# Retention's heads and memory attention's queries and keys turned by transposing DMAs in place of TensorE, and the first key group rotated earlier

## The chip, the cores and the metric

The kernel runs on one core of one Trainium2 chip. A core has TensorE (PE in the profile: matrix products; PEld are its weight loads), VectorE (DVE), ScalarE (ACT), GpSimd (POOL) and SyncE (SP), which here only issues DMAs; 16 DMA engines move data between the device's memory (DRAM) and the on-chip memory (SBUF). Products land in a small accumulator memory (PSUM). The metric is the device time of one execution in microseconds (us); lower is better.

## The reference, cut to what matters

One decoder layer on 256 tokens of width 2048 in float32. The parts that the change touches are the retention mixer's heads on their way into a projection, and the queries and keys of the attention over 256 memory tokens:

```python
hn = rmsnorm(h, norm_mix_w)
q, k, v, g_ret, xr, yr, g_a, g_b = jnp.split(hn @ w_in, offsets, axis=-1)
q = rotary(q, positions); k = rotary(k, positions) * RET_QK_DIM ** -0.5      # 8 heads of 128
ret = head_groupnorm(chunkwise_retention(q, k, v), ret_gn_w).reshape(b, s, D_RET_V)
ret_out = jax.nn.silu(g_ret) * ret                                            # 8 heads of 256
rnn_out = jax.nn.gelu(yr) * rg_lru(causal_dwconv(xr, ...), ...)
merged = sigmoid(g_a) * (ret_out @ w_proj_ret) + sigmoid(g_b) * (rnn_out @ w_proj_rnn)
h = h + merged @ w_mix_out
# attention over the memory, 4 heads of 512
q = rmsnorm(h, norm_xa_w) @ xa_w_q;  k = mem_n @ xa_w_k;  v = mem_n @ xa_w_v
p = softmax(q k^T * 512 ** -0.5);    h = h + (p v) @ xa_w_o
hn = rmsnorm(h, norm_ffn_w); h = h + (silu(gate) * val) @ ffn_w_down          # a causal conv before the gate
out = rmsnorm(h, final_norm_w)
```

## The kernel before, in words

**Precision.** Each float32 operand is split in two parts, hi (a cast) and lo (the remainder, operand minus hi), and a product is hi*hi + hi*lo + lo*hi. ScalarE makes hi of each piece of weights (L285), VectorE makes lo (L286). `split_pair` (L543) does the same for activations, two blocks of 128 features at a time.

**Weights.** All weights come from DRAM as one stream of 1 MB pieces, `in_wall`, in the order of a plan. `prefetch` issues the load of a piece on SP (L264) into one of six raw buffers, and the splits into one of three hi and three lo buffers; it stays two units (`AHEAD`) ahead of the products. In a projection with two blocks of 512 columns (`pair_products`), some products are saved by adding pieces of weights and of activations first: a second piece is added to a raw buffer by a DMA on GpSimd (L266) or by VectorE, and the products read sums of activations (`ss`, made by `sums`). Such a pair has eleven units, seven short ones (q1 to q7, 12 matmuls) and four long ones (p0 to p3, 24 matmuls). Other projections go by four long units.

**Order.** The program is written once in straight order. `later(n, fn)` puts a piece of side work n+1 units later; after each unit those that are due are written out. A scheduler then places instructions on each engine; every engine, and SP's queue, works in order, so one that waits holds what stands behind it.

**Rows and columns.** A projection with `pair_out` gives rows (tokens on partitions), and an operand of the next product must have features on partitions. `transposed` (L523) turns 128x128 blocks on TensorE with an identity matrix (`cid`), four at a time into a PSUM tile `sm` (L529). It is used for:

- retention's heads: `finish_head` (L747) turns a normalised head `rc` (256 tokens x 256), scales it by the group norm's weights into `hd` (L752), and stores it to DRAM; `ret`, a list of the class `Kept`, loads each pair of blocks again (`kt`, L739) while the gates of the merge are computed, splits it, and for the first four also makes the sums that the pair projection needs;
- the queries: `keep` (L1118) turns `o`, copies it to `qc` (L1121), and stores it to DRAM (`qs`, also `Kept`), to be loaded as `kt` before the softmax;
- the keys: `turn_key` (L1135) turns `o` and splits straight out of PSUM (L547, L548 with `sm` as the input), and asks for the softmax two units after the second half;
- the merged rows (`sig` and `o` of the gates) and the residual rows (`nat`), which stay.

**Group 0 of retention.** Queries and keys of four heads are computed with features on partitions, joined (`q`, L540), and rotated by position on VectorE (`rotated`, L715 to L721, then `split_pair`). For group 0, keys: the sums of x (`sum_x`) are put into the four units of the value projection that follows, then comes that projection, and the rotation is written after it, before the values are split (`split_rows`, L562 and L563). The score products (`scores`, L517, `sm<-s,s`) read the rotated keys.

Of the kernel before, what the change touches and what calls it, by code (L numbers as in the profile page):

```python
# [9 lines left out]
F32 = mybir.dt.float32  # L10
F32R = mybir.dt.float32r
I32 = mybir.dt.int32
AF = mybir.ActivationFunctionType
ALU = mybir.AluOpType
AX = mybir.AxisListType

P = 128
D = 2048
S = 256
# [134 lines left out]
def hybrid_layer(  # L154
# [37 lines left out]
    def tmp(s="t"):  # L192
        return tp.tile([P, 2, S], F32, tag="tmp", name=nm(s))
# [109 lines left out]
    def later(n, fn):  # L303

        pending.append((step[0] + n + 1, fn))
# [217 lines left out]
    def transposed(rows):  # L523

        for k in range(0, rows.shape[2], 2 * P):
            t = small()
            for j in range(2):
                for tt in range(2):
                    pe.transpose(  # L529
                        t[:, j, tt * P : (tt + 1) * P], rows[:, tt, k + j * P : k + (j + 1) * P], ident  # L530
                    )
            yield t
# [175 lines left out]
    def rotated(qs_):  # L708

        o = []  # L710
        cb = cos[:, None, :].to_broadcast([P, 2, S])
        for pr in range(2):
            q = qs_[pr]
            ta, tb = tmp("ta"), tmp("tb")
            dve.tensor_tensor(out=ta, in0=q, in1=cb, op=ALU.mult)  # L715
            for lo_, hi_ in ((0, 64), (64, 128)):
                dve.tensor_tensor(  # L717
                    out=tb[lo_:hi_], in0=q[64 - lo_ : 128 - lo_],
                    in1=sin[64 - lo_ : 128 - lo_, None, :].to_broadcast([64, 2, S]), op=ALU.mult,
                )  # L720
            dve.tensor_add(ta, ta, tb)  # L721
            o.append(split_pair(ta))
        return o

    class Kept(list):
# [4 lines left out]
        def store(self, t):  # L730

            sp.dma_start(out=self.rows[self.stored], in_=t)
            self.stored += 1
# [8 lines left out]
                    self.sums.append(sums(t, self.scale))  # L742
            return list.__getitem__(self, i)

    ret = Kept("ret")

    def finish_head(g, hh, raw):  # L747
        for t in transposed(raw):
            c = tmp("hd")
            for j in range(2):  # L750
                i = g * 8 + hh * 2 + j
                act.activation(c[:, j, :], t[:, j, :], AF.Identity, scale=half_gn[:, i : i + 1])  # L752
            ret.store(c)

    def retain(g, qr, kr, vs, dec, gates):

# [73 lines left out]
    for g in range(2):  # L830
        dec = big([P, 4, S], s="dec")
        vs, turned = [], []
        for b, o in enumerate((O_Q, O_K)):
            a = qjoin if g == b == 0 else [joined(t, "q") for t in gemm_t("w_in", 0, xs, NT, o + g * BW)]
            if b == 0:
                sp.dma_start(
                    out=dec,
                    in_=consts[:, C_DEC + g * 4 * S : C_DEC + (g + 1) * 4 * S].rearrange("p (h s) -> p h s", s=S),
                )
            if g > 0:  # L840
                turned.append(rotated(a))
# [271 lines left out]
        done[0] += 1  # L1113
        act.copy(pT, t)

    qs = Kept("qs", None, False)

    def keep(o, pr, kept):  # L1118
        for t in transposed(o[:, :, pr * S : (pr + 1) * S]):
            c = tmp("qc")  # L1120
            act.copy(c, t)  # L1121
            kept.store(c)
# [12 lines left out]
    def turn_key(b, o, pr, ks):  # L1135
        for t in transposed(o[:, :, pr * S : (pr + 1) * S]):
            ks.append(split_pair(t))
        if pr == 1:
            later(1, lambda: softmax([qs[2 * b], qs[2 * b + 1]], ks))

    for b in (0, 2):
        for i in range(KC):
            later(4 + 2 * i, lambda i=i: qs[2 * b + i])
        for i, o in enumerate(pair_out("xa_w_k", ms, ms.sums, b * BW, rsms[0])):
            ks = []
            for pr in range(2):
                later(1 + 3 * i + pr, lambda b=b + i, o=o, pr=pr, ks=ks: turn_key(b, o, pr, ks))
    osp, osp_sums = [], []

    def attend(b, v):  # L1150
# [194 lines left out]
```

## Time and profile before

| | |
|---|---|
| median of 3 runs | 2006.2 us (2006.16 to 2008.58) |
| the profiled execution's own time | 2005.55 us |
| its span in the profile | 2003.8 us |
| granted TensorE clock | 0.999 |
| moved by DMA | 443.57 MB, 221 GB/s over the span |

In a group's row stand the line, engine, operation, output<-input by the program's names, partitions x elements, the count, then busy us and the mean ns of one, then the engine's idle time before them and what ended it. In a timeline's row stand the start, the busy time, the engine, the line and, in brackets, the idle time before it and what ended that. Matmuls overlap: one of 512 columns lasts about 0.39 us and the next starts 0.23 us after it began. A DMA row has its size and the median time from issue to landing. A stretch's row has its length, then the busy us (and count) of PE, PEld, DVE, ACT and POOL, the clock, the mean busy share of the DMA engines, and GB/s.

### The profile page before, as it was taken

Reading aid. Unit: us, or ns where it says so; the run is one execution under the profiler, and the core shown is the slowest. Engines: PE = TensorE matmul, PEld = TensorE weight load, DVE = VectorE, ACT = ScalarE, POOL = GpSimd, SP = SyncE. Lnnn points to the kernel's source line nnn. Section 1 sums busy time; section 2 is a strip of 40 time slices with the busy share of each in tenths; the row PEclk is TensorE's granted clock in tenths of the full one; section 3 lists DMA queues with packets and bytes.
Section 4 is the critical chain, followed back from the end, with each engine's and each line's share of the span. In section 5 each row is a group of like instructions: output and inputs, shape, how many; then the busy total and the mean of one; then the engine's idle time right before and its main releaser. Section 6 shows DMA issues by size and latency. Waiting matters only on the chain.

```text
span 2003.8 us, 24972 instructions
## 1 busy us (share of the span) xinstructions
PE 1988.4 (99%) x10072; PEld 1692.9 (84%) x10072; DVE 1583.4 (79%) x1588; ACT 1157.9 (58%) x1167; POOL 47.0 (2%) x52
## 2 busy tenths in 40 slices
PE   9999999999999999999999999999999999999998
PEld 8878888888888888888888888888888888888887
DVE  6798797789985876778888768777797787886775
ACT  6565656767665554566666656555554554544552
POOL 0001000000000000000000000000000000000000
PEclk9999999999999999999999999999999999999999
DMA  9764675555887675777886748754678555684561
GB/s 370 259 214 135 235 257 179 210 190 157 266 261 261 210 252 183 248 257 234 267 259 206 258 126 231 264 198 174 207 233 275 196 192 216 204 290 178 204 237 64
DMA packets 79460, 443.57 MB, mean 221 GB/s; under 512 B 8688, under 2 KB 13424, under 8 KB 31600
## 3 DMA queue, kind: packets, MB, share of 16 engines
q1 hardware_dynamic: 72064, 397.39, 53.9%
q0 software_dynamic: 5760, 41.95, 11.2%
q10 hardware_dynamic: 1520, 2.63, 0.4%
q8 instruction: 79, 1.29, 0.3%
q14 instruction: 37, 0.30, 0.0%
HBM read 425.16 MB, written 16.78 MB: 221 GB/s over the span
## 4 chain that ended last, share of the span: by engine, by line
PE 91%; DVE 3%; issue 2%; DMA 2%; ACT 1%; POOLq 0%; SPq 0%; ACTq 0%; POOL 0%; DVEq 0%
PE acc L350 38%; PE acc L361 16%; PE acc L368 16%; PE acc L362 16%; DMA raw<-in_wall 2%; PE sm L517 2%; DVE lo L286 1%; PE sm L529 1%; PE acc L517 1%; ACT hi L285 1%; PE sm L894 1%; DVE raw L293 0%; DVE tb L717 0%; DVE ta L721 0%; DVE fv L1192 0%
## 5 line engine op out<-in xcount | busy, mean ns | idle before, releaser
L286 DVE TENSOR_TENSOR lo<-raw,hi 128x2048 fp32r<-128x2048 f32 (+1 forms) x420 | 951.0, 2267 | 295.0 <-ACT hi L285 288.1
L285 ACT CAST hi<-raw 128x2048 fp32r<-128x2048 f32 (+1 forms) x418 | 793.2, 1902 | 615.5 <-PE acc L362 274.2
L361 PE MATMUL acc<-hi,s 128*128 128x512 f32 x1336 | 522.6, 391 | 2.0 <-DVE v L563 1.6
L362 PE MATMUL acc<-hi,s 128*128 128x512 f32 x1336 | 520.7, 390 | 0.4 <-DVE s L551 0.4
L350 PE MATMUL acc<-s,hi 128*128 128x512 f32 x2176 | 519.3, 392 | 1.1 <-DVE hi L283 1.1
L350 PEld LDWEIGHTS acc<-s,hi 128*128 128x128 f32 x2176 | 402.7, 189 | 80.9 <-issue 1.4
L368 PE MATMUL acc<-lo,s 128*128 128x512 f32 x1336 | 340.0, 392 | 0.0
L361 PEld LDWEIGHTS acc<-hi,s 128*128 128x128 f32 x1336 | 250.9, 188 | 54.6 <-DVE v L563 2.0
L368 PEld LDWEIGHTS acc<-lo,s 128*128 128x128 f32 x1336 | 250.1, 188 | 53.3
L362 PEld LDWEIGHTS acc<-hi,s 128*128 128x128 f32 x1336 | 250.9, 188 | 52.2 <-DVE s L551 1.1
L350 PEld LDWEIGHTS acc<-s,lo 128*128 128x128 f32 x2176 | 277.7, 192 | 8.8 <-DVE lo L286 0.4
L350 PE MATMUL acc<-s,lo 128*128 128x256 f32 x2176 | 282.9, 284 | 0.0
L361 PE MATMUL acc<-hi,ss 128*128 128x512 f32 x320 | 126.4, 395 | 1.8 <-ACT o L453 1.5
L362 PE MATMUL acc<-hi,ss 128*128 128x512 f32 x320 | 124.8, 390 | 0.0
L368 PE MATMUL acc<-lo,ss 128*128 128x512 f32 x320 | 86.0, 390 | 0.0
L539 ACT COPY c<-acc 128x512 f32<-128x512 f32 x68 | 39.4, 581 | 70.3 <-PE acc L350 69.9
L361 PEld LDWEIGHTS acc<-hi,ss 128*128 128x128 f32 x320 | 60.1, 188 | 16.0 <-ACT o L453 2.0
L266 POOL DMA_DIRECT2D raw<-in_wall x40 | 35.2, 879 | 1570.3 <-DVE lo L286 999.0
L368 PEld LDWEIGHTS acc<-lo,ss 128*128 128x128 f32 x320 | 60.0, 188 | 12.7
L362 PEld LDWEIGHTS acc<-hi,ss 128*128 128x128 f32 x320 | 60.1, 188 | 12.1
L426 DVE TENSOR_TENSOR nat<-nat,acc 128x512 f32<-128x512 f32 (+1 forms) x49 | 43.9, 908 | 5.1 <-PE acc L368 5.1
L291 DVE TENSOR_TENSOR raw<-raw,raw 128x2048 f32<-128x2048 f32 x20 | 45.8, 2288 | 0.4
(233 smaller groups left out, 1241.8 us busy)
## 6 DMA issues: line engine op xcount, KB each, us to landing
raw<-in_wall SPq DMA_DIRECT2D x333, 1024.0 KB, 4.9
raw<-in_wall POOLq DMA_DIRECT2D x40, 1024.0 KB, 7.9
fkept<-nat SPq DMA_DIRECT2D x12, 512.0 KB, 7.5
nat<-fkept SPq DMA_DIRECT2D x12, 512.0 KB, 5.8
xt<-in_x_t SPq DMA_DIRECT2D x11, 256.0 KB, 6.5
raw<-in_wall SPq DMA_DIRECT2D x5, 512.0 KB, 7.9
nat<-in_x ACTq DMA_DIRECT2D x4, 512.0 KB, 10.0
ret<-hd SPq DMA_DIRECT2D x8, 256.0 KB, 4.1
```

The costliest lines, as they stand in the source:

```text
L266: pool.dma_start(out=raw, in_=src, accum_op=ALU.add)
L285: act.copy(hi[:, a:b], raw[:, a:b])
L286: dve.tensor_tensor(out=lo[:, a:b], in0=raw[:, a:b], in1=hi[:, a:b].bitcast(F32), op=ALU.subtract)
L291: dve.tensor_tensor(out=to, in0=to, in1=by, op=ALU.add)
L350: pe.matmul(a, part, sx, start=k == 0 and t == 0, stop=k == nk - 1 and t == 0, skip_group_check=True)
L361: pe.matmul(o, h, hi, start=start and kk == 0, stop=False, skip_group_check=True)
L362: pe.matmul(o, l, hi, start=False, stop=False, skip_group_check=True)
L368: pe.matmul(o, h, lo, start=False, stop=stop and kk == KC - 1, skip_group_check=True)
L426: dve.tensor_tensor(out=o, in0=o, in1=i, op=op)
L517: pe.matmul(o, a, b, start=start and i == 0, stop=stop and i == 2, skip_group_check=True)
L529: pe.transpose(t[:, j, tt * P : (tt + 1) * P], rows[:, tt, k + j * P : k + (j + 1) * P], ident)
L539: act.copy(c, a[:, :, S:BW])
```

## The change

A float32 word is treated as two 16-bit halves. `planes` writes rows as two planes of halves, upper and lower, by two ScalarE copies of 16-bit values with a stride of two; a transposing DMA (`dma_start_transpose`, issued on SP) turns 128-column blocks of 16-bit values; `join_planes` puts the halves of two blocks together again with two ScalarE copies.

- Heads and queries: a new class `KeptRows` stores the planes of 512 columns (512 KB) to DRAM, and its first use of an even index loads and turns 512 KB at once into a tile `d`; two joins make two pairs of blocks. For the heads, the scaling by the group norm's weights moves behind the join (on ScalarE, in place).
- Keys: the planes are turned within the SBUF, in two transposing DMAs of 128 tokens each; the two joins come three and four units after the planes, the softmax five.
- Group 0: `rotated` for the keys is written before the sums of x and the value projection.

```diff
+    def words(t):
+        return t.bitcast(U16).rearrange("p t (w two) -> p t w two", two=2)
+    def planes(t, rows, cs=slice(0, BW)):
+        for i in range(2):
+            act.copy(t[:, :, i, cs], words(rows)[:, :, :, 1 - i])
+    def join_planes(d, pr):
+        t = tmp("jp")
+        for i in range(2):
+            act.copy(words(t)[:, :, :, 1 - i], d[:, i, 2 * pr : 2 * pr + 2, :])
+        return t
+    class KeptRows(list):
...
+        def store(self, b, t):
+            sp.dma_start(
+                out=self.rows[b].rearrange("(t p) c -> p t c", p=P), in_=t.rearrange("p t a w -> p t (a w)")
+            )
+        def __getitem__(self, i):
+            while len(self) <= i:
+                k = len(self)
+                if k % 2 == 0:
+                    self.turned = big([P, 2, KC, S], U16, s="d")
+                    sp.dma_start_transpose(
+                        out=self.turned.rearrange("p a c s -> p (a c) s"), in_=self.rows[k // 2]
+                    )
+                t = join_planes(self.turned, k % 2)
+                if self.wcol is not None:
+                    for j in range(2):
+                        act.activation(t[:, j, :], t[:, j, :], AF.Identity, scale=self.wcol(2 * k + j))
+                self.append(split_pair(t))
+                if self.wcol is not None and len(self) <= KC:
+                    self.sums.append(sums(t))
...
     def finish_head(g, hh, raw):
-        for t in transposed(raw):
-            c = tmp("hd")
-            for j in range(2):
-                i = g * 8 + hh * 2 + j
-                act.activation(c[:, j, :], t[:, j, :], AF.Identity, scale=half_gn[:, i : i + 1])
-            ret.store(c)
+        if hh % 2 == 0:
+            head_rows[0] = big([P, 2, 2, BW], U16, s="hr")
+        planes(head_rows[0], raw, slice((hh % 2) * DV, (hh % 2 + 1) * DV))
+        if hh % 2 == 1:
+            ret.store(2 * g + hh // 2, head_rows[0])
...
                 if b == 1:
+                    turned.append(rotated(a))
                     for i in range(KC):
                         later(i, lambda i=i: sum_x(i))
                 v = gemm_n("w_in", 0, xs, NT, O_V + b * BW)
-                turned.append(rotated(a))
+                if b == 0:
+                    turned.append(rotated(a))
                 vs.append(split_rows(v, rs0))
...
-            for pr in range(2):
-                later(1 + 2 * i + pr, lambda o=o, pr=pr: keep(o, pr, qs))
+            later(1 + 2 * i, lambda b=b + i, o=o: qs.store(b, row_planes(o)))
...
-    def turn_key(b, o, pr, ks):
-        for t in transposed(o[:, :, pr * S : (pr + 1) * S]):
-            ks.append(split_pair(t))
-        if pr == 1:
-            later(1, lambda: softmax([qs[2 * b], qs[2 * b + 1]], ks))
+    def turn_key(b, o):
+        rows = row_planes(o)
+        d = big([P, 2, KC, S], U16, s="d")
+        for tt in range(2):
+            sp.dma_start_transpose(
+                out=d.rearrange("p a c s -> p (a c) s")[:, :, tt * P : (tt + 1) * P],
+                in_=rows[:, tt].rearrange("p a w -> p (a w)"),
+            )
+        ks = []
+        for pr in range(2):
+            later(2 + pr, lambda pr=pr: ks.append(split_pair(join_planes(d, pr))))
+        later(4, lambda: softmax([qs[2 * b], qs[2 * b + 1]], ks))
```

`row_planes` allocates a tile `rp` and calls `planes` on it. The keys are asked for at `later(1 + 2 * i)` in place of `later(1 + 3 * i + pr)`.

More of the change, by code (lines that the diff above doesn't have):

```diff
@@ L12 @@
 I32 = mybir.dt.int32
+U16 = mybir.dt.uint16
 AF = mybir.ActivationFunctionType
@@ L743, in __getitem__, with __init__ @@
             return list.__getitem__(self, i)
-    ret = Kept("ret")
-    def finish_head(g, hh, raw):
-        for t in transposed(raw):
-            c = tmp("hd")
-            for j in range(2):
-                i = g * 8 + hh * 2 + j
-                act.activation(c[:, j, :], t[:, j, :], AF.Identity, scale=half_gn[:, i : i + 1])
-            ret.store(c)
+    def words(t):
[9 more added lines that the diff above has]
+    class KeptRows(list):
+        def __init__(self, name, wcol=None):
+            self.rows = dp.tile([4, S, 2 * BW], U16, name=name)
+            self.wcol, self.sums, self.turned = wcol, [], None
+        def store(self, b, t):
[17 more added lines that the diff above has]
+                    self.sums.append(sums(t))
+            return list.__getitem__(self, i)
+    ret = KeptRows("ret", lambda i: half_gn[:, i : i + 1])
+    head_rows = [None]
+    def finish_head(g, hh, raw):
+        if hh % 2 == 0:
[3 more added lines that the diff above has]
+            ret.store(2 * g + hh // 2, head_rows[0])
     def retain(g, qr, kr, vs, dec, gates):
@@ L1114, in transpose_probs, with row_planes @@
         act.copy(pT, t)
-    qs = Kept("qs", None, False)
-    def keep(o, pr, kept):
-        for t in transposed(o[:, :, pr * S : (pr + 1) * S]):
-            c = tmp("qc")
-            act.copy(c, t)
-            kept.store(c)
+    qs = KeptRows("qs")
+    def row_planes(o):
+        t = big([P, 2, 2, BW], U16, s="rp")
+        planes(t, o)
+        return t
     for b in (0, 2):
@@ L1144, in hybrid_layer @@
         for i, o in enumerate(pair_out("xa_w_k", ms, ms.sums, b * BW, rsms[0])):
-            ks = []
-            for pr in range(2):
-                later(1 + 3 * i + pr, lambda b=b + i, o=o, pr=pr, ks=ks: turn_key(b, o, pr, ks))
+            later(1 + 2 * i, lambda b=b + i, o=o: turn_key(b, o))
     osp, osp_sums = [], []
```

1 line of the change is left out of this document (removed).

## The prediction

> **What bounds the kernel now.** I read the page first (span, busy shares, chain), then the groups of instructions by line, then TensorE's timeline where the change cuts, then the issues of the DMA queues and the busy time by stretch. From the page: the span, TensorE's share, the chain's shares by engine, and how busy the 16 DMA engines are in 40 slices.
>
> ```profile
> span 2003.8 us, 24972 instructions
> PE 1988.4 (99%) x10072; PEld 1692.9 (84%) x10072; DVE 1583.4 (79%) x1588; ACT 1157.9 (58%) x1167; POOL 47.0 (2%) x52
> ...
> DMA  9764675555887675777886748754678555684561
> ...
> PE 91%; DVE 3%; issue 2%; DMA 2%; ACT 1%; POOLq 0%; SPq 0%; ACTq 0%; POOL 0%; DVEq 0%
> ```
>
> TensorE is 91% of the chain and never far from work; ScalarE has 42% of the span free; the DMA engines are mostly at 50 to 80%. So work taken off TensorE is worth its full time while nothing new makes TensorE wait, and work put on ScalarE or the DMA engines is free only while it stays ahead of TensorE. The sum is made against the profiled execution's own 2005.55 us (span 2003.8 us and 1.75 us around it). It lies 0.65 us under the median of the runs, 2006.2 us. About 0.2% (4 us) is what a measurement of this kernel can tell from no change.
>
> The groups that the change touches, by line (count, busy us, mean ns):
>
> ```profile
> L286 DVE TENSOR_TENSOR lo<-raw,hi 128x2048 fp32r<-128x2048 f32 (+1 forms) x420 | 951.0, 2267 | 295.0 <-ACT hi L285 288.1 <-PE acc L368 3.3 <-ACT s L573 1.3
> L285 ACT CAST hi<-raw 128x2048 fp32r<-128x2048 f32 (+1 forms) x418 | 793.2, 1902 | 615.5 <-PE acc L362 274.2 <-issue 132.4 <-PE acc L350 110.6
> ...
> L539 ACT COPY c<-acc 128x512 f32<-128x512 f32 x68 | 39.4, 581 | 70.3 <-PE acc L350 69.9
> ...
> L529 PE MATMUL sm<-cid,o 128*128 128x128 f32 x80 | 12.0, 272 | 0.0
> ...
> L547 ACT CAST s<-kt 128x512 fp32r<-128x512 f32 x16 | 9.8, 624 | 1.6 <-DMA kt<-qs 1.6
> ...
> L752 ACT ACTIVATE hd<-sm,pb 128x256 f32<-128x256 f32 x16 | 6.2, 476 | 0.0
> ...
> L1121 ACT COPY qc<-sm 128x512 f32<-128x512 f32 x8 | 4.7, 587 | 1.0 <-PE sm L529 0.9
> ...
> L547 ACT CAST s<-sm 128x512 fp32r<-128x512 f32 x8 | 4.7, 586 | 0.7 <-PE sm L529 0.7
> ...
> L529 PE MATMUL sm<-cid,rc 128*128 128x128 f32 x32 | 4.1, 272 | 0.0
> ```
>
> The transposes that go are the 32 from rc (retention's heads) and 64 of the 80 from o: 32 of queries, 32 of keys. The other 16 turn the merged rows and stay. 96 go, in 24 sets of four.
>
> **The transposes taken off TensorE.** The 272 ns is a duration that overlaps its neighbours. The cost is what a set adds to the row of starts, from TensorE's timeline in the query projection (start, us):
>
> ```profile
> 947.40 0.39 PE L361 MATMUL acc<-hi,s 128*128 128x512 f32 x1
> ...
> 950.12 0.39 PE L361 MATMUL acc<-hi,s 128*128 128x512 f32 x1
> ...
> 953.74 1.98 PE L368 MATMUL acc<-lo,s 128*128 128x512 f32 x8
> 955.56 0.60 PE L529 MATMUL sm<-cid,o 128*128 128x128 f32 x4
> 955.91 0.48 PE L361 MATMUL acc<-hi,ss 128*128 128x512 f32 x1
> 956.23 0.39 PE L362 MATMUL acc<-hi,ss 128*128 128x512 f32 x1
> 956.46 0.40 PE L361 MATMUL acc<-hi,ss 128*128 128x512 f32 x1
> ```
>
> Matmuls start 0.23 us apart (956.23 to 956.46). From the set's start at 955.56 to the second matmul behind it, 956.23, pass 0.67 us, where one matmul would take 0.23: a set costs 0.44 us. 24 sets x 0.44 = 10.6 us off the path. TensorE has no gap here that hides them, so all of it is gained if no wait comes.
>
> The Trainium skill, "TensorE: Matmul & The Clock Gate", Part 4 (PE-mode transpose), gives about 275 ns for a 128x128 transpose in a kernel's context; taken as a cost, 96 would be worth 26 us. This trace has the same 272 ns as a duration and 0.11 us as the cost; the measurement decides.
>
> **The keys of group 0 rotated sooner.** What TensorE does where that rotation ends now:
>
> ```profile
> 106.63 1.07 PE L368 MATMUL acc<-lo,ss 128*128 128x512 f32 x4
> 107.54 0.63 PE L517 MATMUL sm<-s,s 128*128 128x256 f32 x4
> 109.06 1.12 PE L517 MATMUL sm<-s,s 128*128 128x256 f32 x8 [0.89 <-DVE s L548]
> 111.37 0.50 PE L361 MATMUL acc<-hi,ss 128*128 128x512 f32 x1 [1.20 <-ACT o L453]
> ...
> 113.32 1.07 PE L368 MATMUL acc<-lo,ss 128*128 128x512 f32 x4
> 115.99 0.50 PE L361 MATMUL acc<-hi,s 128*128 128x512 f32 x1 [1.60 <-DVE v L563]
> ```
>
> Four score products at 0.12 us should end at 108.02: the next start at 109.06, 1.04 us late, for the split of the rotated key. The eight should end at 110.02, and 111.37 is 1.35 us late: ScalarE's copy stood behind the key's cast. The four at 113.32 should end at 114.23, and 115.99 is 1.76 us late: the values' split stood behind the rotation, so their accumulator was not free. Together 4.15 us, the largest waits after the start. VectorE around it:
>
> ```profile
> 78.31 0.68 DVE L540 TENSOR_TENSOR q<-acc,c 128x512 f32<-128x512 f32 x1
> 80.67 2.29 DVE L286 TENSOR_TENSOR lo<-raw,hi 128x2048 fp32r<-128x2048 f32 x1 [1.68 <-ACT hi L285]
> ...
> 100.45 0.68 DVE L715 TENSOR_TENSOR ta<-q,cos 128x512 f32<-128x512 f32 x1
> ...
> 101.37 1.38 DVE L717 TENSOR_TENSOR tb<-q,sin 64x512 f32<-64x512 f32 x2
> 102.78 0.69 DVE L506 TENSOR_TENSOR ss<-sm,ss 128x512 fp32r<-128x512 f32 x1
> ```
>
> The keys are joined at 78.99 and turned only from 100.45. Moved up, two rotations with their splits (2 x (0.68 + 1.38 + 0.68 + 0.68) = 6.8 us) push what VectorE does behind them by up to 6.8 us, less its idle time there (1.68 us before the row at 80.67 alone). What is late next are the four sums of x: the last one ends at 103.47, and the first product that reads all four starts at 104.8. In the changed kernel's order TensorE has the twelve score products ahead of it, some 2 us, so the last sum may come 3.4 us later than now. That about covers what is left of the 6.8. Gain between 0 and 4.15 us, and a loss of up to 3.4 (6.8 - 3.4) if no idle time absorbs anything: I take a gain of 3.0, nearest to the rows, as all three waits name the moved chain.
>
> **What ScalarE gets.** By the 512-column copy (581 ns) and, halfway to the 2048-column cast (1902 ns), 1.02 us for 1024 columns. Heads: planes 16 x 0.58 = 9.3 and 7.7 of scaling later, for the 7.6 of the hd rows; joining 16 x 0.58 = 9.3: +18.7 us. Queries: planes 8 x 1.02 = 8.2, joining 9.3, less 8 x 0.587 = 4.7: +12.8. Keys: planes 8.2, joining 9.3, casts 624 for 586 ns: +17.8. Together +49 us. If 16-bit copies cost half or twice, 25 to 90; I take the equal cost. VectorE's splits stay 683 for 679 ns: nothing. Its load by stretch:
>
> ```profile
> 980.00:1020.00 40.00, 40.00 (x186) 33.07 (x185) 36.71 (x31) 27.63 (x29) 1.76 (x2) 1.00 0.86 268
> ...
> 1060.00:1100.00 40.00, 40.00 (x196) 33.34 (x195) 32.24 (x30) 24.49 (x28) 1.75 (x2) 1.00 0.65 203
> ```
>
> The fourth busy number is ScalarE's: 24 to 28 of 40 us, and the 31 us of queries and keys fall over some 190 us: 61 to 69% become about 80%. The average fits. But ScalarE works in order, and up to eleven copies and casts stand together in front of a cast that TensorE needs. Three buffers hold split weights, so a cast may start two or three units of TensorE's ahead; units are 2.72 us (947.40 to 950.12) and 5.44 us (950.12 to 955.56). At the first key group's end the order is: a cast, eleven copies and casts of 0.6 us, a cast: 1.9 + 6.5 + 1.9 = 10.3 us against 2.72 + 5.44 + 2.72 = 10.9 us. It fits, with 0.6 us over.
>
> **What the queues get.** SP's issues, with us to landing:
>
> ```profile
> raw<-in_wall SPq DMA_DIRECT2D x333, 1024.0 KB, 4.9
> ...
> ret<-hd SPq DMA_DIRECT2D x8, 256.0 KB, 4.1
> ...
> kt<-ret SPq DMA_DIRECT2D x8, 256.0 KB, 6.6
> ...
> kt<-qs SPq DMA_DIRECT2D x8, 256.0 KB, 5.6
> nat<-hkept SPq DMA_DIRECT2D x4, 512.0 KB, 6.9
> ...
> rgw<-in_rg_w_a SPq DMA_DIRECT2D x4, 256.0 KB, 5.4
> ...
> pa<-in_by_feature ACTq DMA_DIRECT2D x1, 8.0 KB, 2.4
> ```
>
> Stores become 8 of 512 KB for 16 of 256 KB; 16 loads of 256 KB become 8 transposing loads of 512 KB; the keys add 8 transposing moves of 256 KB within the SBUF. Eight issues fewer, 2 MB more of 444. They share SP's queue with the weights; in the changed order six raw buffers keep the loads several units ahead, so a store that waits for ScalarE's planes holds nothing urgent.
>
> No row shows a transposing DMA. Lower bound: an ordinary one, 6.9 us for 512 KB, 5.6 for 256 KB. Upper bound: its 16 blocks of 128x128 one after the other, each at the smallest DMA's 2.4 us: 38 us. The 256 KB of rgw in 512-byte pieces land in 5.4 us, as fast as long rows, so short pieces alone do no harm: I take about 8 us, near the lower end. Cover: at the tightest place (second key block of the first group, and the query behind it in the queue) planes end about 4 us after a short unit, and the first join stands 12.8 us after it (5.44 + 2.72 + 2.72 + the cast's 1.9): 8.8 us. Elsewhere 7 to 12. So most land in time, some by a hair. For new waits from ScalarE and late landings I take 4 us, between 0 and the 28 of the first rival below.
>
> The sum: -10.6 - 3.0 + 4 = -9.6 us: 1995.9 us against the profiled 2005.55, 1996.6 against the median; I give 1996.5.
>
> **Rivals.**
> 1. *Slower: the transposing DMAs outlast their cover.* A join then stands on ScalarE with the weights' casts behind it. It decides when the twelve tiles (four of heads, of queries, of keys) cost 13.6 / 12 = 1.1 us each, at a landing near 10.5 us (8.8 + 0.6 over above + 1.1). For it: DMA engines 86% busy in the stretch quoted above, and the keys' two moves and a 512 KB one in a row. Against: the two to three units by which ScalarE leads at the other places. At 14 us (twice the 6.9), 5.2 us over, 4.6 after the 0.6, at the six tight tiles (the keys' four and two queries behind them): +28, so 2006.2 - 13.6 + 28 = 2021 us.
> 2. *The same, block by block.* At 21 us a tile (between 6.9 and 38) all twelve are about 9 us late: +108, so 2101 us. "VectorE: DVE Perf Modes", "The three transpose paths", in the Trainium skill has 1309 ns for a 128x128 block by DMA, 21 us for 16 in turn (an estimate); "Advanced Engine Details and Errata", X-Bar Transpose, says such DMAs run about as fast as plain ones, at 350 to 400 GB/s, which would leave the forecast. No row here shows either.
> 3. *ScalarE takes TensorE's place.* The joins hold back casts by 1 to 3 us in each of about six dense blocks: +12 us in place of the 4, so 2006.2 - 13.6 + 12 = 2004.6 us, no change to speak of.
> 4. *The rotation brings nothing,* because the scores wait for something else: 2006.2 - 10.6 + 4 = 1999.6 us, still faster.
>
> **How the numbers follow.** Forecast with rival 4: 0.60. Rival 3: 0.13, of which 0.10 within 0.2% and 0.03 above. Rival 1: 0.22; rival 2: 0.05. So faster 0.60, same 0.10, slower 0.30. The likeliest case's own range is 1991.5 (no new wait, all 4.15) to 2002 (0.2% under the median); the range for 8 in 10 is 1990 to 2024, through rival 1 and short of rival 2.
>
> **What would show it.** Right: transposes from o 16 and none from rc on TensorE; no wait over 0.5 us at 107 to 116; landings of the transposing moves under 10 us; ScalarE near 1207 us busy; its joins not waiting for DMA. Wrong: ScalarE's joins waiting several us for a transposing DMA, TensorE then waiting for hi or lo at 520 to 610 and 1000 to 1150; or SP's weight loads landing later.

## The result and the profile after

| | before | after |
|---|---|---|
| median (16 runs each) | 2006.34 us | 2011.92 us |
| lowest to highest | 2005.55 to 2008.58 us | 2007.31 to 2023.9 us |
| the profiled execution's own time | 2005.55 us | 2008.96 us |
| its span | 2003.8 us | 2007.2 us |

The ratio over the runs is 1.0037, 95% interval 1.0022 to 1.0053 (the medians alone stand at 1.0028): slower, where 1996.5 us and a gain were forecast. The changed kernel's times also scatter over 16.6 us, those of before over 3.0. The profiled execution lies near the low end of that scatter.

The page after the change: span, busy shares, DMA packets, and the chain's shares by engine.

```profile
span 2007.2 us, 24826 instructions
PE 1982.7 (99%) x9976; PEld 1686.3 (84%) x9976; DVE 1584.6 (79%) x1588; ACT 1207.6 (60%) x1239; POOL 47.0 (2%) x52
...
DMA packets 102115, 445.65 MB, mean 222 GB/s; under 512 B 33392, under 2 KB 38128, under 8 KB 54256
...
PE 89%; DVE 4%; DMA 3%; ACT 2%; issue 1%; SPq 1%; POOLq 0%; ACTq 0%; DVEq 0%
```

TensorE has 96 matmuls fewer and ScalarE 49.7 us more, as worked out. But the kernel waits more, and of 102115 packets 33392 are under 512 bytes (8688 of 79460 before).

Where the time came from, by excess: for each matmul, how much later the next one starts than is usual behind one of its kind, added up in stretches of 20 us. It grows by about 2 us at 100 to 120, 1.1 at 640 to 660, 8.5 at 1040 to 1080 and 1.0 at 1120 to 1140, and over the whole kernel by about 12, against 10.6 saved. That gives some 1.4 of the 3.4 us by which the spans differ; the rest is not accounted for. So two places matter.

**The pause at 1057 us.** In the kernel before, TensorE is busy throughout this stretch:

```profile
1040.00:1060.00 20.00, 20.00 (x109) 17.06 (x108) 16.63 (x12) 12.02 (x11) 0.86 (x1) 1.00 0.60 174
```

The changed kernel's timeline of SP's queue there (start, time, line, move):

```profile
1018.63 19.32 SPq L265 DMA_DIRECT2D raw<-in_wall  x5
1038.00 9.84 SPq L1185 DMA_TRANSPOSE d<-rp  x4
1047.90 8.91 SPq L778 DMA_TRANSPOSE d<-qs  x1
1056.92 18.45 SPq L265 DMA_DIRECT2D raw<-in_wall  x5
```

From 1038.00 to 1056.81 the queue issues transposing DMAs, or waits to, and no weight. ScalarE's timeline of the same kernel:

```profile
1049.83 1.26 ACT L456 ACTIVATE o<-acc,ro 128x512 f32<-128x512 f32 x2
1056.33 1.90 ACT L286 CAST hi<-raw 128x2048 fp32r<-128x2048 f32 x1 [5.24 <-DMA raw<-in_wall]
1058.91 2.00 ACT L759 COPY jp<-d 128x512 uint16<-128x512 uint16 x3 [0.67 <-DMA d<-qs]
1060.79 0.60 ACT L548 CAST s<-jp 128x512 fp32r<-128x512 f32 x1
```

And TensorE's:

```profile
1056.84 0.39 PE L362 MATMUL acc<-hi,s 128*128 128x512 f32 x1
1063.20 0.58 PE L518 MATMUL sm<-s,s 128*128 128x256 f32 x1 [5.98 <-ACT s L548]
1063.58 0.63 PE L363 MATMUL acc<-hi,s 128*128 128x512 f32 x1
1064.01 0.63 PE L362 MATMUL acc<-hi,s 128*128 128x512 f32 x1
```

In brackets stand the wait and what released it. ScalarE stood 5.24 us for a weight that POOL's queue had asked for at 1046.13 with an adding transfer (`raw<-in_wall`, the weight's summand added into the buffer by DMA). The joins come behind that cast, the first of them waits 0.67 us more for the query block, and TensorE, which wants the scores, stands 6 us. The query block landed at 1058.9 (issued at 1047.90, 11.0 us), so with the weight in time the first join could still not have begun sooner: both transfers were late, and the query's ended last. Then TensorE's matmuls start 0.43 us apart in place of 0.23: half clock. The stretches, with the clock third from the end (a DMA packet is counted whole in the stretch in which it starts, so that the share of the DMA engines, the last number but one, can pass 1):

```profile
1056.00:1060.00 4.00, 1.22 (x6) 0.68 (x4) 1.73 (x1) 2.99 (x3) 0.00 (x0) 1.00 1.14 265
1060.00:1064.00 4.00, 0.80 (x2) 0.71 (x3) 2.61 (x4) 4.00 (x8) 0.00 (x0) 0.72 1.01 420
1064.00:1068.00 4.00, 4.00 (x15) 3.50 (x14) 1.32 (x2) 4.00 (x6) 0.00 (x0) 0.50 0.62 260
```

The adding and transposing DMAs issued at 1036 to 1053, with the median us to landing at the end. Of the kernel before:

```profile
raw<-in_wall POOLq DMA_DIRECT2D x1, 1024.0 KB, 7.6
```

Of the changed kernel:

```profile
raw<-in_wall POOLq DMA_DIRECT2D x1, 1024.0 KB, 10.1
d<-rp SPq DMA_TRANSPOSE x4, 7.9
d<-qs SPq DMA_TRANSPOSE x1, 11.0
```

The adding transfer takes 2.5 us longer than the same one before, though other adding transfers of the kernel before take up to 10.9 us. The query block's transposing DMA takes 11.0 us where I had counted on 8. So does the first query block's, issued at 999.44 with no keys' DMA near it; an adding transfer was issued 3.8 us behind that one.

**The rotation at 108 us.** TensorE's timeline in the changed kernel:

```profile
106.59 1.50 PE L518 MATMUL sm<-s,s 128*128 128x256 f32 x12
108.66 0.49 PE L363 MATMUL acc<-hi,ss 128*128 128x512 f32 x1 [0.57 <-DVE ss L507]
112.32 0.51 PE L362 MATMUL acc<-hi,ss 128*128 128x512 f32 x1 [3.17 <-ACT ss L506]
```

Its stretches there, with the clock third from the end:

```profile
108.00:112.00 4.00, 0.58 (x2) 0.19 (x1) 4.00 (x9) 0.35 (x1) 0.04 (x1) 1.00 0.00 0
112.00:116.00 4.00, 3.46 (x8) 2.56 (x9) 2.65 (x7) 3.82 (x6) 0.83 (x1) 0.61 0.69 98
```

All twelve score products now run at once, so the keys come in time. But TensorE then waits 0.7 and 3.43 us for the sums of x (`ss`), and the clock is halved for 3.4 us behind it. From VectorE's timeline, a sum of weights and, last, the fourth sum of x:

```profile
109.13 2.29 DVE L294 TENSOR_TENSOR raw<-raw,raw 128x2048 f32<-128x2048 f32 x1
...
112.30 0.69 DVE L507 TENSOR_TENSOR ss<-sm,ss 128x512 fp32r<-128x512 f32 x1 [0.15 <-ACT ss L506]
```

### The profile page after: what moved, and what is told of

Same layout as the page of the kernel before. It is cut to its first block, busy times and chain, and to the rows that moved or that the text cites. A ratio compares the mean times of both kernels' runs of the same rounds, so it can differ in the third digit from the quotient of the medians.

```text
span 2007.2 us, 24826 instructions
## 1 busy us (share of the span) xinstructions
PE 1982.7 (99%) x9976; PEld 1686.3 (84%) x9976; DVE 1584.6 (79%) x1588; ACT 1207.6 (60%) x1239; POOL 47.0 (2%) x52
## 2 busy tenths in 40 slices
DMA packets 102115, 445.65 MB, mean 222 GB/s; under 512 B 33392, under 2 KB 38128, under 8 KB 54256
## 4 chain that ended last, share of the span: by engine, by line
PE 89%; DVE 4%; DMA 3%; ACT 2%; issue 1%; SPq 1%; POOLq 0%; ACTq 0%; DVEq 0%
PE acc L351 37%; PE acc L363 16%; PE acc L369 16%; PE acc L362 16%; DMA raw<-in_wall 2%; DVE lo L287 2%; PE sm L518 2%; ACT hi L286 1%; PE acc L518 1%; PE sm L941 1%; DVE raw L294 1%; DMA d<-qs 1%; PE sm L530 1%; SPq L1185 0%; ACT jp L759 0%
```

## The experiments

Times are medians; ratios are over the runs, to the kernel before, run on the same chip, with the 95% interval. The experiments were spread over several chips, so differences between their times carry that too.

**The four parts alone.** Each is the kernel before with one part of the change: `finish_head` and `ret = KeptRows(...)`; the rotation's line; `qs = KeptRows("qs")`; `turn_key`.

> Retention's heads alone by planes and transposing DMAs; queries, keys and the rotation as before. Theory A (the loss sits in two places, the third query block behind the keys' transposing DMAs on SP, and the rotation): the eight sets of four transposes come off TensorE with no wait of note, 8 x 0.44 = 3.5 us faster than before, 2002 to 2004 us. Theory B (a cost at every tile, by ScalarE's joins and by SP held 4.3 us per transposing load): no gain or up to 3 us slower, 2006 to 2009 us.

> The keys of group 0 rotated sooner, alone. Theory A (the wait is only handed on to the sums of x, and a pause of over 3 us brings a stretch of half clock): no gain, 0 to 5 us slower than before, 2006 to 2011 us. Theory B (the rotation gains what the prediction gave it, and the tiles alone lose): 3 to 4 us faster, 2002 to 2003 us.

> The queries alone by planes and transposing DMAs, the keys turned on TensorE. Theory A: with no transposing keys in front of them on SP, the four query loads land in time and 8 sets x 0.44 us are gained: 3.5 us faster than before, 2002 to 2004 us, no pause of TensorE over 1 us at 1000 to 1130. Theory B: no gain or up to 4 us slower, as each load holds SP for 4 to 5 us.

> The keys alone by planes and transposing DMAs within the SBUF, the queries turned on TensorE and loaded as before. Theory A: SP is held 5 us by four keys' moves instead of 18.9 us by them and a query load, so the softmax waits 0 to 3 us instead of 6: between 3.5 us faster and even, 2002 to 2007 us. Theory B: 2 to 6 us slower, with the softmax waiting for the keys' joins.

| part alone | median | ratio | range |
|---|---|---|---|
| heads | 2003.98 us | 0.9988 (0.9979 to 0.9997) | 2002.7 to 2004.6 |
| rotation | 2008.67 us | 1.0013 (1.0003 to 1.0022) | 2007.1 to 2011.4 |
| queries | 2002.89 us | 0.9983 (0.9973 to 0.9992) | 2001.8 to 2006.3 |
| keys | 2009.21 us | 1.0015 (1.0006 to 1.0025) | 2008.0 to 2012.4 |

The kernel before had 2006.49 us beside them. Heads and queries gain 2.5 and 3.6 us, rotation and keys lose 2.2 and 2.7. The sum is -1.2 us, the whole change is +5.6 (2011.92 - 2006.34): some 6.8 us and the wide scatter come only of the parts together. The loss of the keys alone is in their trace as five pauses of 1.1 to 1.5 us between 1053 and 1123, 6.1 us in all against 3.5 saved: at the first, TensorE waits for ScalarE, which had stood 2.53 us at a join for the keys' DMA.

**Ordinary DMAs in place of the transposing ones.**

```diff
-            sp.dma_start_transpose(
+            sp.dma_start(
                 out=d.rearrange("p a c s -> p (a c) s")[:, :, tt * P : (tt + 1) * P],
-                in_=rows[:, tt].rearrange("p a w -> p (a w)"),
+                in_=rows[:, tt].rearrange("p a (c s) -> p (a c) s", s=P),
```

> The changed kernel with every transposing DMA replaced by ordinary DMAs of the same bytes into the same tiles (the halves land unturned, so the scores of memory attention and retention's heads are not those of the reference). Stores, planes, joins, queue order, rotation: as in the changed kernel. Theory A (the loss is what the transposing DMAs do: they hold SP's queue for 18.9 us at 1038 to 1057 and weight loads behind them come late, TensorE pauses 6.1 us and then runs 6.8 us at half clock): the held stretch shrinks to under 2 us, the pause goes, and the time falls by 7 to 10 us to 2000 to 2004 us. Theory B (the loss comes from the 96 planes and 48 joins on ScalarE, 49.7 us of added work, wherever the data come from): the time stays at that of the changed kernel, 2008 to 2013 us.

2010.44 us, ratio 1.0019 (1.0009 to 1.0029), 2008.7 to 2013.1. No 7 to 10 us gained: theory A falls as it was put. (The copies into planes are 32, not 96 as that expectation says; the 49.7 us are the measured difference.) In its trace a move is issued in 0.6 to 0.9 us (medians), so SP was not held, yet the query's two land 9.9 us after issue, and TensorE still paused 3.37 us at 1064. It moves the same 256-byte pieces (6353 packets under 512 bytes at 1035 to 1070, 6416 in the changed kernel). What it lost less at 1057, it lost more in the heads' stage: 4.5 us of pauses at 648 to 653 for 0.96 in the changed kernel.

**Heads and queries; the rotation with the sums; the queries sooner.**

> Heads and queries by transposing DMA, keys turned on TensorE, rotation as before. Theory A (keys and queries disturb each other on SP's queue, nothing else does): the gains of the two parts alone add, 2.5 and 3.5 us, so 2000 to 2001.5 us, ratio about 0.997. Theory B (each transposed tile costs by itself on ScalarE): two parts together cost more than each alone, 2004 us or more.

> The kernel before with the first group's keys rotated sooner, as in the change, and the four sums of x put ahead too, into the units of the second half of the key projection. If the rotation's gain was only handed to the sums, which are then the last to finish: the waits of 4.2 us at 107 to 113 fall to under 1 us and no half-clock stretch follows, 2001 to 2003 us. If VectorE is simply full there, the wait only moves again: 2005 to 2009 us, as with the rotation alone (2008.7).

> The changed kernel with the queries' transposing DMAs asked for four units sooner, so that the third block's is issued ahead of the keys' four and not behind them. Theory A with the order on SP's queue as the cause: the pause of 6.1 us at 1057 shrinks to under 3 us, 2003 to 2007 us. If the total time for which SP is held matters and not the order: the pause stays within 1.5 us of 6.1, 2008 to 2013 us.

The edit of the second (the first is parts one and three of the table above; the third is `later(2 * i, ...)` for `later(4 + 2 * i, ...)`):

```diff
         for b, o in enumerate((O_Q, O_K)):
+            if g == 0 and b == 1:
+                for i in range(KC):
+                    later(i, lambda i=i: sum_x(i))
             a = qjoin if g == b == 0 else ...
...
                 if b == 1:
                     turned.append(rotated(a))
-                    for i in range(KC):
-                        later(i, lambda i=i: sum_x(i))
```

Heads with queries: 2005.4 us, 0.9992 (0.9982 to 1.0001). A miss: the gains did not add. A new pause of 2.0 us at 1063, where the joins wait 1.57 us for the query block, is in its trace and not in that of queries alone; why it lands later there was not found.

Rotation with early sums: 2001.94 us, 0.9977 (0.9967 to 0.9986). As expected, both waits and the half clock are gone. The same stretches as above, of this kernel:

```profile
108.00:112.00 4.00, 4.00 (x19) 3.32 (x18) 4.00 (x2) 1.39 (x2) 0.87 (x1) 1.00 0.00 0
112.00:116.00 4.00, 4.00 (x19) 3.32 (x18) 3.06 (x3) 2.29 (x2) 0.00 (x0) 1.00 1.04 168
```

Queries sooner: 2014.42 us, 1.0043 (1.0029 to 1.0057). Not better: the order on SP's queue alone is not it. The third block, now ahead of the keys, lands 11.3 us after its issue all the same. In the profiled execution the one pause became three, of 2.65, 0.92 and 2.24 us at 1054 to 1068.

**The keys' DMAs left out; the sums in the whole change.**

```diff
-        for tt in range(2):
-            sp.dma_start_transpose(
-                out=d.rearrange("p a c s -> p (a c) s")[:, :, tt * P : (tt + 1) * P],
-                in_=rows[:, tt].rearrange("p a w -> p (a w)"),
-            )
...
-            later(2 + pr, lambda pr=pr: ks.append(split_pair(join_planes(d, pr))))
+            later(2 + pr, lambda pr=pr: ks.append(split_pair(join_rows(pr))))
```

> The changed kernel without the keys' eight transposing DMAs: the joins read the planes where they lie, unturned (the scores are not those of the reference). Planes, joins, splits and their order on ScalarE stay. Theory C, formed after the ordinary DMAs of 256-byte pieces did not help (the pieces of 256 bytes fill the 16 DMA engines, so that the weight's adding transfer lands 10.1 us after its issue and the query block 11.0 us after, and ScalarE, which works in order, stands on them): the pause of 6.1 us at 1057 falls under 1.5 us, the weight lands within 8.5 us, and the time falls by 5 to 9 us to 2003 to 2007 us. Theory B (the joins themselves, 0.65 us each, are late on ScalarE): the pause stays over 3 us and the time within 3 us of the changed kernel's.

> The changed kernel with the four sums of x put ahead, into the units of the second half of the key projection, and nothing else. If the rotation's wait was only handed to the sums, and this loss stands by itself (rotation alone 2.2 us slower than before, rotation with early sums 4.9 us faster): 6 to 7 us less than the changed kernel, 2004 to 2006 us; the waits of 4.7 us at 107 to 113 and the half clock behind them go, the pause at 1057 stays. If the two losses are not independent (the later one grows as the earlier work comes sooner): 2008 us or more.

Without the keys' DMAs: 2007.36 us, 1.0006 (0.9997 to 1.0016), and 2006.8 to 2009.2 only. The weight lands in 8.0 us; the pause is 2.9 us, twice what I had set. So 4.6 us and nearly the whole scatter go with these eight DMAs. The rest of the pause does not: ScalarE and TensorE in this kernel,

```profile
1054.79 1.91 ACT L286 CAST hi<-raw 128x2048 fp32r<-128x2048 f32 x1 [2.73 <-DMA raw<-in_wall]
1056.61 1.41 ACT L759 COPY jp<-d 128x512 uint16<-128x512 uint16 x2
...
1060.92 0.38 PE L518 MATMUL sm<-s,s 128*128 128x256 f32 x1 [2.74 <-ACT s L548]
```

The weight comes as it does without any keys' DMA (7.6 to 8.9 us in the nine kernels that have none), no join in this burst waits for a DMA, and TensorE still stands 2.9 us for joins and casts in ScalarE's queue. By this run about half of the 6.1 us is ScalarE's own order, which is rival 3.

With the sums ahead: 2004.6 us, 0.9998 (0.998 to 1.0015), 7.3 us less than the change. Its ten runs fall into two groups, 2000.7 to 2005.5 and 2011.5 to 2013.9. The profiled one, 2013.73, is of the upper group. Its adding and transposing DMAs issued at 1036 to 1053:

```profile
raw<-in_wall POOLq DMA_DIRECT2D x1, 1024.0 KB, 21.8
d<-rp SPq DMA_TRANSPOSE x3, 7.0
d<-qs SPq DMA_TRANSPOSE x1, 22.2
```

Its stretches:

```profile
1040.00:1044.00 4.00, 4.00 (x19) 3.30 (x19) 3.96 (x3) 3.29 (x4) 0.18 (x1) 1.00 1.32 64
1044.00:1048.00 4.00, 4.00 (x20) 3.30 (x19) 3.61 (x2) 0.51 (x1) 0.00 (x0) 1.00 1.24 29
1048.00:1052.00 4.00, 2.63 (x12) 1.86 (x10) 0.00 (x0) 0.00 (x0) 0.00 (x0) 1.00 1.58 63
1052.00:1056.00 4.00, 0.00 (x0) 0.00 (x0) 0.00 (x0) 0.00 (x0) 0.00 (x0) 0.96 0.71 88
```

The last two numbers are the DMA engines' share and the GB/s: for 16 us they are put down as busy for 0.71 and more and move 29 to 88 GB/s, and from 1052 to 1060 every engine of the core stands still. The keys' fourth DMA, issued at 1039.33 beside the adding transfer (1039.32), lands with it, after 21.9 us. TensorE's pause is 16.9 us. I call this the jam. That the two groups are executions with and without it is my reading; only this one was profiled.

**Two versions made of the parts that gain.**

> Queries alone by transposing DMA, with the rotation sooner and the sums of x put ahead. If these two gains are independent: 3.4 and 4.9 us add, 1998 us. If the later one takes back what the earlier one gives: 2001 us or more.

> Heads and queries by transposing DMA, keys on TensorE, rotation sooner with the sums of x put ahead. If all three gains add: 1995.5 to 1997 us. If heads and queries together bring no more than either alone, as in the run with these two: 1999 to 2001 us.

Queries, rotation and early sums: 1998.63 us, 0.9962 (0.9947 to 0.9977); the gains add (1998 expected). With the heads too: 1999.8 us, 0.9966 (0.9953 to 0.9979), so heads bring nothing more here.

**What makes the jam: order, or cover.** The first is `later(4 + b + 2 * i, ...)` for the queries, the second `later(6, ...)` for `later(4, lambda: softmax(...))`, the third both with the early sums.

> The changed kernel with the third and fourth query block asked for two units later, so that a weight load goes out on SP's queue between the keys' four transposing DMAs and the query block's. Theory D (the jam: keys' and query block's transposing DMAs, issued one behind the other while a weight's adding transfer is under way, slow each other and that transfer, by 6 us in one execution of the changed kernel and by 17 us in one of the kernel with early sums; without the keys' DMAs it never came): the query block's issue stays under 7 us and its landing under 10 us, no pause of over 4 us, the spread of the runs falls under 5 us and the median to 2005 to 2008 us. If a jam comes wherever a transposing DMA meets an adding transfer: the spread stays over 8 us and the median over 2009 us.

> The changed kernel with the scores of memory attention asked for two units later; DMAs stay where they are. If the loss at 1057 is want of cover (TensorE asks for products whose keys are still in ScalarE's queue): other matmuls fill the time, the pause falls under 2 us and the median to 2004 to 2007 us. Theory D (the weights themselves land late in the jam): TensorE runs out of weights as well, pauses of 3 us or more stay, the spread stays over 8 us and the median over 2008 us.

> The changed kernel with three edits together: sums of x ahead, query blocks two units later, scores two units later. If the losses are the rotation's (6.5 us) and the jam with the want of cover (6 us), all three transposes' gains stand: 1997 to 2000 us with a spread under 5 us. If the joins on ScalarE cost by themselves, 2002 us or more.

Queries apart: 2014.05 us, 1.0031 (1.0016 to 1.0046), 2006.4 to 2019.1. Theory D, that the query block has to stand right behind the keys', falls. In this execution the query's DMA goes out only at 1056.8; the adding transfer, issued at 1047.3, takes 15.7 us and the keys' fourth DMA 16.1. Its adding and transposing DMAs issued at 1036 to 1053:

```profile
raw<-in_wall POOLq DMA_DIRECT2D x1, 1024.0 KB, 15.7
d<-rp SPq DMA_TRANSPOSE x4, 7.3
```

The stretches show that the stall is there before the query's DMA is issued (the last number is GB/s):

```profile
1050.00:1054.00 4.00, 3.20 (x15) 2.31 (x13) 2.29 (x1) 4.00 (x4) 0.00 (x0) 1.00 0.06 11
1054.00:1058.00 4.00, 2.68 (x8) 2.10 (x9) 3.97 (x3) 2.30 (x5) 0.00 (x0) 0.74 0.66 85
```

Scores later: 2015.79 us, 1.0067 (1.0018 to 1.0116), up to 2038.5. Its profiled execution, 2009.99, pauses 4.05 us at 1104 instead: TensorE waits for ScalarE to empty an accumulator, and that stands behind joins which waited 1.12 us for the keys' DMA. The want of cover at one place is moved to another.

All three: 1997.02 us, 0.9961 (0.9941 to 0.9981); three of the five runs lie at 1995.4 to 1997.0, two at 2004.2 and 2005.6. The profiled execution is one of the fast three (1997.02): there all four parts together do gain. They do not gain all: 2007.1 - 10.6 - 4.9 would be 1991.6 us, and its trace still has a pause of 2.60 us at 1046, where TensorE waits for ScalarE, which had stood 3.02 us at a join for the keys' DMA. That the slower two are executions with the jam was not shown.

**The adding transfers.** Of forty, the 26th and 28th meet the keys' DMAs (issued at 1046 and 1104).

```diff
+                    adds[0] += 1
+                    if adds[0] not in (26, 28):
-                    pool.dma_start(out=raw, in_=src, accum_op=ALU.add)
+                        pool.dma_start(out=raw, in_=src, accum_op=ALU.add)
```

> The changed kernel with two of the forty adding transfers left out (the 26th and 28th, issued at 1046 and 1104 us, which meet the keys' transposing DMAs); two blocks of the key projection's weights are then not summed, and the keys are not those of the reference. Theory E (the jam needs a weight's adding transfer, on its own queue, under way together with the keys' transposing DMAs from SBUF): no pause over 3 us at 1040 to 1075, spread under 5 us, median 2003 to 2006 us. If the transposing DMAs jam by themselves or with any weight load: runs still reach 2012 us and more, median over 2008 us.

> Queries and keys by transposing DMA, heads on TensorE and rotation as before. If the jam comes from queries and keys together: it stands here, spread over 6 us, median 2008 us or more, against 2002.9 and 2009.2 us of either alone (2005.5 us if their differences to before merely add). If the earlier parts of the change bring it on: spread under 5 us, 2004 to 2007 us.

> The changed kernel with the same two transfers kept, on the same queue, with the same bytes from HBM, but writing instead of adding (two blocks of the key projection's weights are then the second summand alone, and the keys are not those of the reference). If the jam comes of the adding (a transfer that also reads what it adds to), it goes as when they were left out: median 2003 to 2006 us, spread under 5 us, landing under 9 us. If any 1 MB transfer under way together with the keys' transposing DMAs is enough, or the lateness comes from that queue: median 2008 us or more, landing over 9 us, spread over 6 us.

Left out: 2003.58 us, 0.9986 (0.9977 to 0.9996), 2002.6 to 2005.2. 8.3 us less than the change, and the wide scatter is gone (2.6 us). ScalarE in its trace, with the same joins in the same order:

```profile
1050.47 1.92 ACT L290 CAST hi<-raw 128x2048 fp32r<-128x2048 f32 x1
1052.28 2.04 ACT L763 COPY jp<-d 128x512 uint16<-128x512 uint16 x3
1054.17 0.62 ACT L552 CAST s<-jp 128x512 fp32r<-128x512 f32 x1
1054.68 1.41 ACT L763 COPY jp<-d 128x512 uint16<-128x512 uint16 x2
```

Neither the cast nor a join waits here. The stretch in this kernel, TensorE busy throughout (17.22 of 20 us in the changed one):

```profile
1040.00:1060.00 20.00, 20.00 (x94) 16.26 (x93) 17.74 (x11) 17.49 (x20) 0.00 (x0) 1.00 0.97 248
```

The burst of eight joins fits here, where it began 6.6 us sooner (1052.28 against 1058.91; 0.9 of that is that the keys' DMAs went out sooner). But this cast has no added weight to wait for at all, so the run does not show that the burst would fit behind a transfer of the usual 8 us; the kernel without the keys' DMAs shows that it does not. Nor is every wait gone. The fourth query block, issued at 1068.35, takes 9.9 us to land beside another adding transfer, issued at 1070.81, which takes 9.7:

```profile
1078.31 1.40 ACT L763 COPY jp<-d 128x512 uint16<-128x512 uint16 x2 [4.93 <-DMA d<-qs]
...
1085.02 0.45 PE L1159 MATMUL sm<-cid,prob 128*128 128x128 f32 x1 [2.64 <-DVE prob L1152]
```

TensorE pauses 2.8 us there and runs at half clock for 3.4 us, with no keys' DMA under way. The kernel without the keys' DMAs and the one with plain writes have the same pause (2.4 and 3.0 us).

Plain writes in their place: 2006.29 us, 1.0001 (0.9991 to 1.001), 2004.4 to 2009.0, landing in 8.7 us, a pause of 3.9 us. This lies between the two expectations. From 2011.92 to 2006.29, 5.6 us and the long tail go with the adding; from there to 2003.58, 2.7 us go with 1 MB more under way. In its trace the query block still takes 10.0 us to land.

Queries and keys without the rest: 2009.21 us, 1.0015 (1.0006 to 1.0024), 2006.9 to 2012.3, a pause of 5.1 us at 1057. This too lies between: the median as for a jam, the spread (5.4 us) just under the 6 set for it. The pause needs only these two parts (the adding transfer lands in 9.0 us, the query block in 11.2), but of the kernels with the adding transfers and the transposing ones the times over 2013 us came only where heads and rotation were there too. Why, stays open.

## Why the prediction was wrong

Of the sum -10.6 - 3.0 + 4, the first term stood. The second came out as +2.2 (the rotation alone), 5.2 us worse. The third must then have been about 14 us (5.6 + 10.6 - 2.2; an estimate, as the parts do not simply add): it is the larger miss.

- *TensorE's 10.6 us.* Right. Queries cost 8 sets of 0.44 = 3.5 us; alone they gain 3.6, and with rotation and sums 3.3 more (2001.94 to 1998.63). Heads alone gain 2.5 of their 3.5; a new pause of 0.96 us at 646 stands in their trace.
- *ScalarE's +49 us, and that the average fits.* Right in the sum (49.7), in part by luck: the 16-bit copies by halves took 0.77 us for joins and 0.62 for the heads' planes, not 0.58, and what made up for it was not traced. That the order fits, "10.3 us against 10.9 us", did not hold: the sum lets the first cast start when ScalarE is free, but it waited for its weight. Without the keys' DMAs, with the weight 8.0 us after its issue, TensorE still stood 2.9 us for the joins. So rival 3 named a real cost at this place, about half of the pause; it was not shown to cost anything in the other dense blocks.
- *"I take a gain of 3.0" for the rotation.* The step that named its limit was right and its size wrong. "What is late next are the four sums of x" is what happened. I gave them 3.4 us of room and at most 6.8 us of delay, and took a gain. The last sum ends at 112.99 in place of 103.47, 9.5 us later: the 6.8 us of rotation and a 2.29 us sum of weights (L294) that now stands ahead of it make 9.1. The loss of 2.2 us alone is within the bound I gave, but on the other side of zero; moving the sums too makes it -4.9 (2001.94, with 2006.85 for the kernel before beside it).
- *"I take about 8 us, near the lower end" for the landing, cover 8.8.* This is the step that failed most, with the 4 us for new waits that rest on it, and so did its ground, "short pieces alone do no harm". The moves landed in 7 to 8 us where one part stood alone (medians: heads 7.2, queries 8.2, keys 6.9), but at the place I had named as tightest in 11.0, over the 10.5 at which rival 1 decides, and in 22.2 in another execution. Missing was what stands beside them: POOL's adding transfer, of which I counted neither the place nor the slowing. It went from 7.6 to 10.1, 15.7 and 21.8 us, and the weight's cast on ScalarE with it. Query blocks beside an adding transfer were late without the keys, too: 11.0 us at 999 in the changed kernel, 9.9 at 1068 with the two adds left out, though 5.9 at 1000 with queries and keys alone.
- *"Eight issues fewer", "a store that waits holds nothing urgent".* Incomplete: SP is held while it issues. One transposing DMA of 512 KB takes 4.3 to 8.9 us of SP's time in the changed kernel, one of 256 KB 1.2 to 5.6. Ordinary DMAs without that hold did not run better as a whole, though the pause there fell from 6.1 to 3.4 us; they lost more in the heads' stage. So the hold alone does not explain the loss.
- *The clock.* Not in the sum at all. Each of the two large waits brought half clock, 3.4 and 6.8 us long, the second beginning inside the wait. With starts 0.43 for 0.23 us apart, that is about 1.6 us lost in the first, and 2.5 in the 5.4 us of the second in which TensorE ran.
- *Rival 1* named the right place and direction. Its 2021 us took six tiles late by 4.6 us each; in the profiled execution one place was late by 6, and others are beyond 2020 us. That the result lies inside the range of 1990 to 2024 us is owed to this rival. *Rival 2* (21 us a tile) fell: twelve tiles never came in turn that late.

The Trainium skill, "Advanced Engine Details and Errata", X-Bar Transpose, has such DMAs at 350 to 400 GB/s. Here 512 KB in 7.2 us are 73 GB/s, with issue and receipt in the time; no run here had them alone on the DMA engines. The Trainium skill, "TensorE: Matmul & The Clock Gate", Part 1, says that the clock is judged in windows of about 3.4 us and halved after an idle one: the half-clock stretches of 3.4 and 6.8 us, behind pauses of 3.43 and 6.14 us, agree. The half clock with heads alone (last section), behind waits of 1.06 and 1.36 us, is not covered by it.

## What to carry to other kernels

A DMA in small pieces is priced by what else is under way when it runs, not by its landing alone: list every transfer in flight at the tightest place, those of other queues above all, and ask who waits for each of them if it takes twice as long. Work moved ahead on an engine that runs in order must be followed to the next consumer of everything it is moved past; here moving four small sums along turned a loss of 2.2 us into a gain of 4.9. Times that scatter by 17 us around a profile that looks only 3 us worse say that the profiled execution shows a mild case: profile a neighbour that hits the bad one. And a copy that fits by the sum of an engine's work must also be placed behind whatever that engine waits for.

## What the runs showed of the hardware

- In single executions, the keys' transposing DMAs from SBUF together with an adding DMA moved as little as 29 GB/s for 4 us (with the query's transposing DMA under way) and 11 GB/s (before it was issued). At this place the adding one took 7.6 to 8.9 us in the nine kernels without keys' DMAs and 8.4 to 21.8 with them; elsewhere in the kernel before it took up to 10.9. As a plain write it took 8.7. Why they slow each other was not shown.
- Where the fourth of the keys' transposing DMAs (256 KB) at this place was issued within 1.2 us of the adding one, it took 8.3 to 21.9 us and landed about when that one did; with the adding transfer left out, it took 4.0. Beside the plain write it took 9.5.
- A transposing DMA holds the queue that issues it: medians of 4.3 us (heads, 512 KB) and 1.25 us (keys, 256 KB), once 20.2 us in the jam.
- Half clock also came after shorter waits. With heads alone and in the kernel before, TensorE is busy for 1.91 of the 4 us from 108 to 112; the next 4 us ran at a mean clock of 0.63 with heads alone and at 1.00 in the kernel before.
